# A two-layer encoder trunk: the scan's next operands are loaded after the head norm's store, and in the last head pair two kinds of load wait for steps of the chain

## The chip, the cores and the metric

The kernel runs on one core of a Trainium2 chip. A core has five engines, each with its own instruction queue that is worked through in order: TensorE (PE in the profile, with PEld for its weight loads), VectorE (DVE), ScalarE (ACT), GpSimd (POOL) and SyncE (SP). SyncE computes nothing here; it issues nearly all DMAs, so its queue is the order in which transfers begin. A DMA that waits for a semaphore holds up every DMA behind it in that queue. The metric is the device time of one execution in microseconds.

## The reference

The input x is 512 tokens by 1024 channels. Layer 0 is windowed attention with 16 heads, layer 1 is RWKV-7 time mixing with a forward and a backward scan; each is followed by a gated FFN with a convolution over three tokens. The change touches the time mixing alone, whose core is

```
step:  sa    = state @ a_t
       state = state * w_t + sa (x) b_t + v_t (x) k_t
       y_t   = state @ r_t
y   = scan(forward) + scan(backward)
out = (groupnorm(y) * lnx_w + lnx_b + bonus) * g
x   = x + out @ w_o
```

with 16 heads of 64 channels, all in float32.

## The kernel before, in words

The heads go two at a time, as a pair of 128 channels, so the scan has eight pairs (0 to 7). A pair's 512 tokens are cut into eight chunks of 64, and the chunked form needs, before the chain of steps can run: masked products of the operands (`low`, line 934, masked on VectorE at line 936 into tile `bw`), the inverse of 32 triangular blocks (`solve`, lines 998 and 1000, alternating between GpSimd and VectorE; its input `X` and its result go through DRAM as `ls` and `zs`, since they change partitions), two levels of matmuls with it (`inverses`, `level`), the sums over a pair's sides (`sides`, tile `xa`) and the batches of line 1069 and line 1078 (`batch`). Then eight steps (`step`) carry the state `st` from chunk to chunk: a matmul into a bank (line 1114), and a scaled copy on ScalarE (line 1117). Last is the head norm (`head_norm`, parts n0 to n4), whose result `t` part n4 stores to DRAM as `os` (line 1159).

These parts are laid out by hand. `run` goes over the pairs i, and for every step j it works through the words of `K.between[j]`: `c` is the step of pair i itself; `l0` to `l3` are `low` for pair i+2; `G`, `V` and `g` are rounds of `solve`; `n0` to `n4` are the norm of pair i-1; `p` (`prep`, lines 917 and 918) loads the operands `bk` and `ar` of pair i+3, 1 MB each, from DRAM. After `run`, all its instructions are tied together engine by engine, so that each engine, SyncE too, keeps the order in which they were written. Pair i+3, loaded in turn i, is first used by word `l0` in the first slot of turn i+1: the first of the matmuls at line 934 waits for both loads.

From turn 1 to turn 4 the turn has both a load (`p`) and a store (`n4`). Turns -1 and 0 load but have no norm, turn 5 and later have nothing left to load.

In the last turn (i = 7) `last` adds what the output projection needs: it loads x back from DRAM (`xs`, line 1414, 2 MB), and the generator `heads` loads the stored `os` of pair after pair (line 1424) and splits each into a high and a low part (`oh` on ScalarE, line 97, `ol` on VectorE), once per step from step 1 on. The projection's weights (`wo`, 448 KB each, loaded at line 55) are split likewise (`whi`, line 68; `wlo`, line 71). These weight blocks are written after `run` and are not tied to its order: the compiler's scheduler places their loads, casts and matmuls among the instructions of the last turn.

Of the kernel before, what the change touches and what calls it, by code (L numbers as in the profile page):

```python
# [11 lines left out]
AF = mybir.ActivationFunctionType  # L12
# [37 lines left out]
                        mybir.DependencyInfo(mybir.DependencyClass.NoSync, mybir.DependencyReason.DATA), reason="order")  # L50


def load(K, src, cols):
    raw = K.wraw.tile([P, 1024], F32, name="wraw")[:, :cols]
    K.nc.sync.dma_start(out=raw, in_=src)
    return raw


def weights(K, src, cols, lo_engine, raw=None):

    nc = K.nc
    if raw is None:
        raw = load(K, src, cols)
    hi = K.whi.tile([P, 1024], F32R, name="whi")[:, :cols]
    lo = K.wlo.tile([P, 1024], F32R, name="wlo")[:, :cols]
    K.nw += 1
    if K.wh[K.nw % len(K.wh)] == "C":
        nc.scalar.copy(out=hi, in_=raw)  # L68
    else:
        nc.vector.tensor_copy(out=hi, in_=raw)  # L70
    lo_engine.tensor_tensor(out=lo, in0=raw, in1=hi.bitcast(F32), op=ALU.subtract)  # L71
    return hi, lo


def ahead(K, blocks):

    raws = [load(K, *b[:2]) for b in blocks[:2]]
    nxt = weights(K, *blocks[0], raws[0])
    for i in range(len(blocks)):
        cur = nxt  # L80
        if i + 2 < len(blocks):
            raws.append(load(K, *blocks[i + 2][:2]))
        if i + 1 < len(blocks):
            nxt = weights(K, *blocks[i + 1], raws[i + 1])
        yield cur
# [10 lines left out]
def split(K, hi, lo, src, lo_engine):  # L96
    K.nc.scalar.copy(out=hi, in_=src)  # L97
    lo_engine.tensor_tensor(out=lo, in0=src, in1=hi.bitcast(F32), op=ALU.subtract)


def mm3(K, ps, lhs, rhs, first, last):

    nc = K.nc
    nc.tensor.matmul(ps, lhsT=lhs[0], rhs=rhs[0], start=first, stop=False)  # L104
    nc.tensor.matmul(ps, lhsT=lhs[0], rhs=rhs[1], start=False, stop=False)  # L105
    nc.tensor.matmul(ps, lhsT=lhs[1], rhs=rhs[0], start=False, stop=last)  # L106
# [709 lines left out]
def rwkv_scan(K, A, sc, mid):  # L816

    nc = K.nc
# [4 lines left out]
    C = nc.scalar  # L823
    R = Ctx()
# [6 lines left out]
    def er(e):  # L831
        return slice(HD * e, HD * e + HD)
# [14 lines left out]
    def mk(shape, name, bufs=1, dt=F32):  # L847
        pool = mid if name in MID else pools[next((k for k, v in PLACE.items() if name in v), "batch")]
        return pool.tile(shape, dt, name=name, tag=name, bufs=bufs)
# [234 lines left out]
    def places(j):  # L1084

        return (j, NC - 1 - j), (j, (NC - 1 - j) ^ 4)
# [11 lines left out]
    def added(ct, c, j):  # L1098

        cc, qq = places(j)  # L1100
        c.S = bank("ch", 2)[:, 0:P].rearrange("p (d s) -> p d s", d=2)
        for d, e in BOTH:
            T.matmul(c.S[er(e), d], lhsT=c.BW[:, qq[d], d, e, P:], rhs=c.VV[:, qq[d], d, e], start=d == 0, stop=j == 0 and d == 1)

    def step(ct, c, j):

        cc, qq = places(j)
        st = c.st if j else None
        last = j == NC - 1
        if j == 0:  # L1110
            added(ct, c, 0)
        if not last:
            for d, e in BOTH if j else ():
                T.matmul(c.S[er(e), d], lhsT=c.MT[qq[d] // 4][er(e), qq[d] % 4, d], rhs=st[er(e), d], start=False, stop=d == 1)
            c.st = mk([P, 2, HD], "st", K.nst)
            for d in range(2):
                C.activation(out=c.st[:, d], in_=c.S[:, d], func=AF.Copy, scale=R.gc[:, ct, j, d:d + 1])
        for d, e in BOTH if j else ():
            T.matmul(c.Y[er(1 - e), cc[d]], lhsT=c.QT[qq[d] // 4][er(e), qq[d] % 4, d], rhs=st[er(e), d],
                     start=False, stop=last and d == 1)  # L1120
        if j < NC - 2:
            added(ct, c, j + 1)
# [142 lines left out]
def body(ctx, tc, A, out, stage=9):  # L1265
    nc = tc.nc
    K = Ctx()
    K.nc = nc
    K.tc = tc
    K.nf, K.no, K.nx1s, K.nbon, K.nslot2, K.nwa, K.nrk, K.nar, K.nbk, K.nrt, K.nbr, K.nl, K.nxa, K.nvv = 3, 5, 32, 2, 6, 1, 1, 2, 2, 2, 4, 2, 2, 2  # L1270
    K.nx, K.ntt, K.ntp, K.nak, K.nx1, K.nmt, K.nst, K.depth = 1, 2, 2, 1, 1, 1, 3, 1
    K.e_r = K.e_k = nc.gpsimd
# [42 lines left out]
    K.begin, K.tail = (2,), ("pl", "", "", "")  # L1315
    K.ny = 2
    K.eng.update(z0="V", z1="V")
    K.between = ("w0 c l0 l1 b0 u g4", "c l2 l3 b1 g4 z X I", "c m1 w1 n0 e", "c n1 t0 t1 G3", "c a0 p n2 V6", "c L0 n3 V6", "c L1 a1 n4 V5", "c x0 x1 m0 G4")
    const = ctx.enter_context(tc.tile_pool(name="const", bufs=1, reuse_waits="tile"))

    @contextmanager
    def streams(n, work=True, side="left", psum=True):
        with ExitStack() as e:
            K.wraw = e.enter_context(tc.tile_pool(name=f"wraw{n}", bufs=3, side=side, reuse_waits="tile"))
            K.whi = e.enter_context(tc.tile_pool(name=f"whi{n}", bufs=2, side=side, reuse_waits="tile"))
            K.wlo = e.enter_context(tc.tile_pool(name=f"wlo{n}", bufs=2, side=side, reuse_waits="tile"))
            if work:
                K.work = e.enter_context(tc.tile_pool(name=f"work{n}", bufs=1, reuse_waits="tile"))
            if psum:
                K.pmm = e.enter_context(tc.tile_pool(name=f"pmm{n}", bufs=2, side=side, space=PSUM, reuse_waits="tile"))  # L1330
            yield
# [41 lines left out]
    def right(name):  # L1373
        return tc.tile_pool(name=name, bufs=1, side="right", reuse_waits="tile")

    def ffn(layer, xT, st, nxt, nst, store):
        conv_ffn(K, layer, st["h"], st["l"], st["acc"], A[f"w_up{layer}"], A[f"w_down{layer}"],
                 residual(xT, nxt, nst, store))

    xs = dram.tile([KT, P, S], F32, name="xs")  # L1380
# [26 lines left out]
    with ExitStack() as end:  # L1407
        ops = ExitStack()

        def last(R):  # L1410

            R.x = end.enter_context(right("x1")).tile([P, KT, S], F32, name="xT")
            for i in range(4):
                nc.sync.dma_start(out=R.x[:, 2 * i:2 * i + 2], in_=xs[2 * i:2 * i + 2].rearrange("k p s -> p k s"))
            end.enter_context(streams(2, False, "right", False))
            hl = ops.enter_context(right("ohl"))
            R.oh = [hl.tile([P, S], F32R, name=f"oh{i}") for i in range(KT)]
            R.ol = [hl.tile([P, S], F32R, name=f"ol{i}") for i in range(KT)]


            def heads():
                for i in range(KT - 1):
                    t = hl.tile([P, S], F32, name="o", tag="o", bufs=2)
                    nc.sync.dma_start(out=t, in_=sc["o"][i])
                    split(K, R.oh[i], R.ol[i], t, nc.vector)
                    yield

            return heads()

        scan.run(last)  # L1430
        xT = scan.x
        n = KT - 1
        for ot, (hi, lo) in enumerate(ahead(K, [(A["wo"][i], n * P, nc.vector) for i in range(KT)])):
            ps = scan.bank()
            for kt in range(n):
                c = slice(kt * P, (kt + 1) * P)
                mm3(K, ps, (hi[:, c], lo[:, c]), (scan.oh[kt], scan.ol[kt]), kt == 0, kt == n - 1)
            nc.vector.tensor_tensor(out=xT[:, ot], in0=xT[:, ot], in1=ps, op=ALU.add)
        hi, lo = weights(K, A["wo7"], KT * P, nc.vector)
        left.close()  # L1440
        with tc.tile_pool(name="act2", bufs=1, reuse_waits="tile") as K.act:
            K.accp = K.work = K.act
            on_tile = residual(xT, "nch1" if stage > 2 else None, st if stage > 2 else None, out if stage == 2 else None)
            for ot in range(KT):
                ps = scan.bank()
                c = slice(ot * P, (ot + 1) * P)
                mm3(K, ps, (hi[:, c], lo[:, c]), (scan.oh[n], scan.ol[n]), True, True)
                on_tile(ot, ps)
            ops.close()
            scan.pre.close()  # L1450
            if stage > 2:
                with tc.tile_pool(name="work2", bufs=1, reuse_waits="tile") as K.work:
                    ffn(1, xT, st, None, None, out)
# [75 lines left out]
```

## Time and profile before

| | |
|---|---|
| median of 3 runs | 1610.0 us (1609.33 to 1611.05) |
| the profiled execution's own time | 1609.2 us |
| its span, first to last instruction | 1607.0 us |
| mean granted TensorE clock | 0.942 of full speed |
| PE busy | 1482.1 us, 92% of the span |
| DVE, ACT, POOL busy | 1033.8, 688.2, 442.5 us |
| DMA | 179.09 MB, 111 GB/s on average |

The span has three parts. Up to about 720 us, and again from about 1226 us on, the big matmuls of attention, projections and FFN keep PE at 90% and more. In between lie the preparation of the scan and the eight turns. The first step of turns 0 to 7 begins at 928.6, 961.1, 994.1, 1026.4, 1062.1, 1096.7, 1130.6 and 1170.6 us. In the turns no engine is full: of the 33.0 us from 961.1 to 994.1 PE is busy for 26.95, DVE for 23.47, ACT for 13.97 and POOL for 11.30. A busy share tells little there; what tells is which wait ends last.

### The profile page before, as it was taken

Reading aid. Unit: us, or ns where it says so; the run is one execution under the profiler, and the core shown is the slowest. Engines: PE = TensorE matmul, PEld = TensorE weight load, DVE = VectorE, ACT = ScalarE, POOL = GpSimd, SP = SyncE. Lnnn points to the kernel's source line nnn. Section 1 sums busy time; section 2 is a strip of 40 time slices with the busy share of each in tenths; the row PEclk is TensorE's granted clock in tenths of the full one; section 3 lists DMA queues with packets and bytes.
Section 4 is the critical chain, followed back from the end, with each engine's and each line's share of the span. In section 5 each row is a group of like instructions: output and inputs, shape, how many; then the busy total and the mean of one; then the engine's idle time right before and its main releaser. Section 6 shows DMA issues by size and latency. Waiting matters only on the chain. (4 is left out here: it accounts for less than half of the span.)

```text
span 1607.0 us, 28495 instructions
## 1 busy us (share of the span) xinstructions
PE 1482.1 (92%) x11612; PEld 1197.7 (75%) x11612; DVE 1033.8 (64%) x1642; ACT 688.2 (43%) x1227; POOL 442.5 (28%) x533
## 2 busy tenths in 40 slices
PE   8999999999999998989986588888699999999999
PEld 7767688888888886767765477777577788888887
DVE  6876447777773348968987657667256677777222
ACT  5576534444432224556544243434344444444111
POOL 2630003222310015425498323322200333221000
PEclk9999999999999999999986589877889999999999
DMA  5200022333333322446536546764532222323331
GB/s 189 78 27 1 13 93 92 102 95 101 96 99 115 99 95 66 133 153 216 186 142 200 168 107 148 157 159 112 172 111 79 92 93 92 103 94 102 105 118 56
DMA packets 108978, 179.09 MB, mean 111 GB/s; under 512 B 49200, under 2 KB 62128, under 8 KB 108848
## 3 DMA queue, kind: packets, MB, share of 16 engines
q1 hardware_dynamic: 108704, 177.27, 36.5%
q8 instruction: 91, 1.49, 0.4%
q14 instruction: 39, 0.32, 0.1%
q10 hardware_dynamic: 144, 0.00, 0.0%
HBM read 142.91 MB, written 34.34 MB: 110 GB/s over the span
## 5 line engine op out<-in xcount | busy, mean ns | idle before, releaser
L68 ACT CAST whi<-wraw 128x1024 fp32r<-128x1024 f32 (+2 forms) x196 | 200.4, 1023 | 275.6 <-PE mm L105 179.7
L71 DVE TENSOR_TENSOR wlo<-wraw,whi 128x1024 fp32r<-128x1024 f32 (+2 forms) x139 | 166.9, 1201 | 183.1 <-ACT whi L68 182.3
L104 PE MATMUL mm<-hl,whi 128*128 128x512 f32 x720 | 281.2, 391 | 1.5 <-DVE xT L1359 0.9
L106 PE MATMUL mm<-hl,wlo 128*128 128x512 f32 x720 | 281.6, 391 | 0.5 <-POOL wlo L71 0.4
L105 PE MATMUL mm<-hl,whi 128*128 128x512 f32 x720 | 281.0, 391 | 0.4 <-DVE hl L92 0.4
L71 POOL TENSOR_TENSOR wlo<-wraw,whi 128x1024 fp32r<-128x1024 f32 x57 | 137.1, 2405 | 413.0 <-ACT whi L68 413.0
L185 DVE SCALAR_TENSOR_TENSOR conv<-upad,par,conv 128x512 f32<-128x512 f32 x88 | 125.6, 1430 | 64.0 <-ACT conv L182 64.0
L106 PEld LDWEIGHTS mm<-hl,wlo 128*128 128x128 f32 x720 | 135.5, 188 | 32.0 <-POOL wlo L71 2.7
L104 PEld LDWEIGHTS mm<-hl,whi 128*128 128x128 f32 x720 | 135.6, 188 | 29.7 <-ACT hl L91 1.3
L105 PEld LDWEIGHTS mm<-hl,whi 128*128 128x128 f32 x720 | 135.5, 188 | 29.3 <-DVE hl L92 1.1
L106 PE MATMUL mm<-gh,wlo 128*128 128x512 f32 x352 | 139.0, 395 | 0.0
L104 PE MATMUL mm<-gh,whi 128*128 128x512 f32 x352 | 139.0, 395 | 0.0
L105 PE MATMUL mm<-gl,whi 128*128 128x512 f32 x352 | 139.0, 395 | 0.0
L97 ACT CAST gh<-gact 128x512 fp32r<-128x512 f32 x44 | 27.3, 621 | 141.3 <-DVE gact L194 141.3
L182 ACT ACTIVATE conv<-upad,par 128x512 f32<-128x512 f32 x88 | 71.6, 815 | 21.5 <-DVE upad L180 21.3
L105 PEld LDWEIGHTS mm<-gl,whi 128*128 128x128 f32 x352 | 66.1, 188 | 16.1
L106 PEld LDWEIGHTS mm<-gh,wlo 128*128 128x128 f32 x352 | 66.1, 188 | 16.1
L998 POOL TENSOR_TENSOR tg<-X,Y 128x56 f32<-128x56 f32 (+16 forms) x129 | 47.2, 366 | 111.7 <-DVE Y L1000 81.2
L104 PEld LDWEIGHTS mm<-gh,whi 128*128 128x128 f32 x352 | 66.1, 188 | 15.9
L187 DVE SCALAR_TENSOR_TENSOR conv<-upad,par,conv 128x512 f32<-128x512 f32 x88 | 70.0, 798 | 3.0
L192 ACT ACTIVATE silu<-conv 128x512 f32<-128x512 f32 x44 | 27.8, 632 | 91.3 <-DVE conv L187 91.3
L106 PE MATMUL mm<-sx,wlo 128*128 128x512 f32 (+1 forms) x144 | 58.8, 409 | 2.9 <-DVE wlo L71 2.9
(334 smaller groups left out, 3110.2 us busy)
## 6 DMA issues: line engine op xcount, KB each, us to landing
wraw<-in_w_up_dram SPq DMA_DIRECT2D x88, 512.0 KB, 3.6
wraw<-in_w_down_dram SPq DMA_DIRECT2D x32, 512.0 KB, 3.5
ars<-tab SPq DMA_DIRECT2D x16, 512.0 KB, 3.0
bks<-tab SPq DMA_DIRECT2D x16, 512.0 KB, 3.2
ar<-ars SPq DMA_DIRECT2D x8, 1024.0 KB, 8.7
bk<-bks SPq DMA_DIRECT2D x8, 1024.0 KB, 6.7
wraw<-in_w_down_dram SPq DMA_DIRECT2D x16, 384.0 KB, 3.2
wraw<-in_w_qkv_dram SPq DMA_DIRECT2D x11, 512.0 KB, 4.3
```

What stands on the lines that cost most here:

```text
L68: nc.scalar.copy(out=hi, in_=raw)
L71: lo_engine.tensor_tensor(out=lo, in0=raw, in1=hi.bitcast(F32), op=ALU.subtract)
L97: K.nc.scalar.copy(out=hi, in_=src)
L104: nc.tensor.matmul(ps, lhsT=lhs[0], rhs=rhs[0], start=first, stop=False)
L105: nc.tensor.matmul(ps, lhsT=lhs[0], rhs=rhs[1], start=False, stop=False)
L106: nc.tensor.matmul(ps, lhsT=lhs[1], rhs=rhs[0], start=False, stop=last)
L182: nc.scalar.activation(out=c, in_=u[:, 1:S + 1], func=AF.Identity, scale=K.par[:, cw + 2 * FT + ch:cw + 2 * FT + ch + 1], bias=K.par[:, cb ...
L185: nc.vector.scalar_tensor_tensor(out=c, in0=u[:, 0:S], scalar=K.par[:, cw + ch:cw + ch + 1], in1=c, op0=ALU.mult, op1=ALU.add)
L187: nc.vector.scalar_tensor_tensor(out=c, in0=u[:, 2:S + 2], scalar=K.par[:, cw + 4 * FT + ch:cw + 4 * FT + ch + 1], in1=c, op0=ALU.mult, op ...
L192: nc.scalar.activation(out=sg, in_=acts[0], func=AF.Silu)
L998: en.tensor_tensor(out=tm, in0=X[:, 0:kx, kx:kx + 1].broadcast_to([P, kx, n]), in1=Y[:, kx:kx + 1, m:16].broadcast_to([P, kx, n]), op=ALU. ...
```

## The change

There are two parts.

First, the word `p` moves from slot 4 of `K.between` to slot 6, behind `n4`. It issues DMAs alone, so no other engine's order changes by it; in SyncE's queue the loads of `bk` and `ar` now stand behind the store `os` of the same turn.

Second, in the last turn. A helper `paced` makes a DMA wait for a given instruction. `step` notes its latest scaled copy of the state as `R.pace`. The load of x, formerly four DMAs ahead of everything, becomes four DMAs inside `heads`: two of the eight tiles of x behind step 1, two behind step 3, two behind step 5 and two behind step 6 (step 7 makes no state). The first three loads of output weights wait for steps 2, 4 and 6, through the list `K.paces`.

```
+def paced(K, later, earlier):
+
+    K.tc.add_manual_dep(later.ins, earlier.ins.name,
+                        mybir.DependencyInfo(mybir.DependencyClass.Sync, mybir.DependencyReason.DATA), reason="pace")
...
 def load(K, src, cols):
     raw = K.wraw.tile([P, 1024], F32, name="wraw")[:, :cols]
-    K.nc.sync.dma_start(out=raw, in_=src)
+    x = K.nc.sync.dma_start(out=raw, in_=src)
+    if K.paces:
+        paced(K, x, K.paces.pop(0))
     return raw
...
-                C.activation(out=c.st[:, d], in_=c.S[:, d], func=AF.Copy, scale=R.gc[:, ct, j, d:d + 1])
+                R.pace = C.activation(out=c.st[:, d], in_=c.S[:, d], func=AF.Copy, scale=R.gc[:, ct, j, d:d + 1])
...
-    K.between = (... "c a0 p n2 V6", "c L0 n3 V6", "c L1 a1 n4 V5", "c x0 x1 m0 G4")
+    K.between = (... "c a0 n2 V6", "c L0 n3 V6", "c L1 a1 n4 p V5", "c x0 x1 m0 G4")
...
             R.x = end.enter_context(right("x1")).tile([P, KT, S], F32, name="xT")
-            for i in range(4):
-                nc.sync.dma_start(out=R.x[:, 2 * i:2 * i + 2], in_=xs[2 * i:2 * i + 2].rearrange("k p s -> p k s"))
...
                     split(K, R.oh[i], R.ol[i], t, nc.vector)
+                    if i % 2 == 0:
+                        paced(K, nc.sync.dma_start(out=R.x[:, i:i + 2], in_=xs[i:i + 2].rearrange("k p s -> p k s")), R.pace)
+                    else:
+                        K.paces.append(R.pace)
                     yield
```

What the built programs' queues show. SyncE's queue in turn 1, before: the loads of a pair's `bk` and `ar` stand between the loads for the norm (`gt`, `bo`) and the norm's store `os`; `ls` is the first store of the next turn.

```order
L1055 DMA gt<-gs 128x512 [waits DMAHW0_49]
L1057 DMA bo<-bos 128x512 [waits DMAHW1_49]
L917 DMA bk_5951<-bks 128x2x1024 [waits DMAHW2_49,PE_49]
L918 DMA ar_7303<-ars 128x2x1024 [waits DMAHW3_49,DVE_49]
L1159 DMA os<-t 128x512 [waits DMAHW4_49,DVE_49]
L942 DMA ls<-bw_7305 32x16x32 [waits DMAHW5_49,DVE_49]
```

The same place now (lines above the change have moved on by 6 or 8):

```order
L1063 DMA gt<-gs 128x512 [waits DMAHW0_49]
L1065 DMA bo<-bos 128x512 [waits DMAHW1_49]
L1167 DMA os<-t 128x512 [waits DMAHW2_49,DVE_49]
L925 DMA bk_5951<-bks 128x2x1024 [waits DMAHW3_49,PE_49]
L926 DMA ar_7303<-ars 128x2x1024 [waits DMAHW4_49]
L950 DMA ls<-bw_7305 32x16x32 [waits DMAHW5_49,DVE_49]
```

The store, which waits for VectorE, now stands ahead of both loads. The same swap is in turns 2, 3 and 4 and nowhere else.

SyncE's queue at the start of the last turn, before (`xT<-xs` is x, `o<-os` a stored pair, `wraw<-in_wo_dram` a block of output weights):

```order
L1159 DMA os<-t 128x512 [waits DMAHW5_49,DVE_49]
L1414 DMA xT<-xs 128x2x512 [waits PE_49,DMAHW6_49,Activation_49,Pool_49]
L1414 DMA xT<-xs 128x2x512 [waits DMAHW7_49]
L1414 DMA xT<-xs 128x2x512 [waits DMAHW0_49]
L1414 DMA xT<-xs 128x2x512 [waits DMAHW1_49]
L1424 DMA o<-os 128x512 [waits DMAHW2_49]
L1055 DMA gt<-gs 128x512 [waits DMAHW3_49]
L1057 DMA bo<-bos 128x512 [waits DMAHW4_49]
L1424 DMA o<-os 128x512 [waits DMAHW5_49]
L55 DMA wraw<-in_wo_dram 128x896 [waits DMAHW6_49]
L55 DMA wraw<-in_wo_dram 128x896 [waits DMAHW7_49]
L55 DMA wraw<-in_wo_dram 128x896 [waits DMAHW0_49]
```

And now, from the DMA behind that `os` on:

```order
L1431 DMA o<-os 128x512 [waits DMAHW6_49,PE_49]
L1434 DMA xT<-xs 128x2x512 [waits PE_49,DMAHW7_49,Activation_49,Pool_49]
L1063 DMA gt<-gs 128x512 [waits DMAHW3_49,DMAHW0_49]
L1065 DMA bo<-bos 128x512 [waits DMAHW4_49,DMAHW1_49]
L1431 DMA o<-os 128x512 [waits DMAHW2_49]
L1431 DMA o<-os 128x512 [waits DMAHW6_49,DVE_49]
L61 DMA wraw<-in_wo_dram 128x896 [waits Activation_49]
L1434 DMA xT<-xs 128x2x512 [waits DMAHW5_49,Activation_49]
L1431 DMA o<-os 128x512 [waits DMAHW2_49,DVE_49]
L1431 DMA o<-os 128x512 [waits DMAHW7_49,DMAHW3_49,DVE_49]
L61 DMA wraw<-in_wo_dram 128x896 [waits DMAHW0_49,Activation_49]
L1434 DMA xT<-xs 128x2x512 [waits DMAHW1_49,Activation_49]
```

The four loads of x are spread out, each with its wait for a step on ScalarE (`Activation`), and the loads of `o` and of weights stand behind them.

ScalarE's queue at the same place, before (`x_...` and `vv` are the copies between the two batches, `st` the states of the steps, `t<-t` a square in the norm):

```order
L904 COPY x_11840<-mm 128x4x64
L68 CAST whi<-wraw 128x896
L904 COPY x_11840<-mm 128x4x64
L904 COPY vv<-mm 64x4x64 x4
L68 CAST whi<-wraw 128x896
L904 COPY x_11865<-pre_5948 128x4x64
L904 COPY x_11865<-pre_5949 128x4x64
L904 COPY vv<-pre_5948 64x4x64 x2
L904 COPY vv<-pre_5949 64x4x64 x2
L1117 ACTIVATE st<-bank,gc 128x64 x4
L97 CAST oh_11930<-o 128x512
L1117 ACTIVATE st<-bank,gc 128x64 x2
```

And now, up to step 4:

```order
L912 COPY x_11840<-mm 128x4x64 x2
L912 COPY vv<-mm 64x4x64 x4
L912 COPY x_11865<-pre_5948 128x4x64
L912 COPY x_11865<-pre_5949 128x4x64
L1125 ACTIVATE st<-bank,gc 128x64 x4
L105 CAST oh_11926<-o 128x512
L1125 ACTIVATE st<-bank,gc 128x64 x2
L105 CAST oh_11927<-o 128x512
L76 CAST whi<-wraw 128x896
L1125 ACTIVATE st<-bank,gc 128x64 x2
L1148 ACTIVATE t<-t 128x512
L105 CAST oh_11928<-o 128x512
```

The two weight casts have left the copies ahead of step 0; the first now stands between steps 2 and 3, the second (not shown) between steps 4 and 5.

## Rows read from the trace of the kernel before

**Rows 1.** Timeline of SyncE, turns 1 to 4: start us, issue us, line, DMA

```profile
978.86 0.38 SPq L917 DMA_DIRECT2D bk<-bks  x1
979.33 0.42 SPq L918 DMA_DIRECT2D ar<-ars  x1
988.81 0.33 SPq L1159 DMA_DIRECT2D os<-t  x1
...
1021.46 0.33 SPq L1159 DMA_DIRECT2D os<-t  x1
...
1054.13 0.33 SPq L1159 DMA_DIRECT2D os<-t  x1
...
1089.32 0.33 SPq L1159 DMA_DIRECT2D os<-t  x1
```

**Rows 2.** DMA view, load at 979.33 (KB, us to landing); then all of line 918

```profile
ar<-ars SPq DMA_DIRECT2D x1, 1024.0 KB, 8.7
...
DMA to landing us min/median/max: 5.2/8.7/10.5
```

**Rows 3.** Timeline of PE: the first masked product of turns 2 to 5

```profile
994.11 0.49 PE L934 MATMUL mm<-ar,bk 64*128 64x128 f32 x4
...
1026.49 0.38 PE L934 MATMUL pre<-ar,bk 64*128 64x128 f32 x2
...
1062.16 0.49 PE L934 MATMUL mm<-ar,bk 64*128 64x128 f32 x4
...
1096.74 0.49 PE L934 MATMUL pre<-ar,bk 64*128 64x128 f32 x4
```

**Rows 4.** Timeline of DVE, turns 2 to 4: copy behind the masks [idle before <-releaser]

```profile
1000.95 0.59 DVE L906 COPY X<-Y 64x512 f32<-64x512 f32 x1 [0.39 <-POOL Y L1000]
...
1033.59 0.59 DVE L906 COPY X<-Y 64x512 f32<-64x512 f32 x1 [0.66 <-POOL Y L1000]
...
1068.64 0.59 DVE L906 COPY X<-Y 64x512 f32<-64x512 f32 x1
```

**Rows 5.** Chain that ended last, turn 1: start us, us, what

```profile
968.05 0.59 DVE X L906
...
972.80 5.13 DMA X<-ls
...
988.09 0.69 DVE t L1155
```

**Rows 6.** Chain that ended last, start of the last turn

```profile
1154.96 8.69 DMA wraw<-in_wo_dram
```

**Rows 7.** Timeline of ACT, last pair

```profile
1153.78 0.37 ACT L904 COPY x<-mm 128x256 f32<-128x256 f32 x1 [1.17 <-PE mm L1069]
1163.73 0.94 ACT L68 CAST whi<-wraw 128x896 fp32r<-128x896 f32 x1 [9.58 <-DMA wraw<-in_wo_dram]
1164.57 0.36 ACT L904 COPY x<-mm 128x256 f32<-128x256 f32 x1
...
1170.61 0.52 ACT L1117 ACTIVATE st<-bank,gc 128x64 f32<-128x64 f32 x2 [1.24 <-PE bank L1103]
...
1175.64 0.52 ACT L1117 ACTIVATE st<-bank,gc 128x64 f32<-128x64 f32 x2 [1.98 <-PE bank L1114]
...
1179.38 0.52 ACT L1117 ACTIVATE st<-bank,gc 128x64 f32<-128x64 f32 x2 [1.16 <-PE bank L1114]
...
1181.99 0.52 ACT L1117 ACTIVATE st<-bank,gc 128x64 f32<-128x64 f32 x2 [1.09 <-PE bank L1114]
```

**Rows 8.** Timeline of PE, last pair: the two batches of line 1078

```profile
1165.63 2.74 PE L1078 MATMUL mm<-bw,x 64*64 64x128 f32 x32 [11.01 <-ACT vv L904]
...
1172.96 1.10 PE L1078 MATMUL pre<-bw,x 64*64 64x128 f32 x32
```

**Rows 9.** Busy us by stretch: PE, PEld, DVE, ACT, POOL, then granted clock, DMA share, GB/s

```profile
1159.90:1165.60 5.70, 0.00 (x0) 0.00 (x0) 0.90 (x1) 1.84 (x4) 0.00 (x0) 0.50 0.78 300
```

**Rows 10.** DMA view: a weight load issued at 1165.82 (KB, us to landing)

```profile
wraw<-in_wo_dram SPq DMA_DIRECT2D x1, 448.0 KB, 3.2
```

More of the change, by code (lines that the diff above doesn't have):

```diff
@@ L1269, in body @@
     K.tc = tc
+    K.paces = []
     K.nf, K.no, K.nx1s, K.nbon, K.nslot2, K.nwa, K.nrk, K.nar, K.nbk, K.nrt, K.nbr, K.nl, K.nxa, K.nvv = 3, 5, 32, 2, 6, 1, 1, 2, 2, 2, 4, 2, 2, 2
@@ L1317, in body @@
     K.eng.update(z0="V", z1="V")
-    K.between = ("w0 c l0 l1 b0 u g4", "c l2 l3 b1 g4 z X I", "c m1 w1 n0 e", "c n1 t0 t1 G3", "c a0 p n2 V6", "c L0 n3 V6", "c L1 a1 n4 V5", "c x0 x1 m0 G4")
+    K.between = ("w0 c l0 l1 b0 u g4", "c l2 l3 b1 g4 z X I", "c m1 w1 n0 e", "c n1 t0 t1 G3", "c a0 n2 V6", "c L0 n3 V6", "c L1 a1 n4 p V5", "c x0 x1 m0 G4")
     const = ctx.enter_context(tc.tile_pool(name="const", bufs=1, reuse_waits="tile"))
```

## The prediction

> **What bounds the kernel now.** I read the chain of waits first, then the timelines of the engines that it names. In the turns the chain runs through the inverse of the triangular blocks: masked products on PE, masks on DVE, the store `ls`, its way back as `X` (5.13 us), the rounds of `solve`, and behind them the norm's last product `t` at 1155, which `os` stores [rows 5]. SyncE's timeline shows the two loads going out about 10 us ahead of that store, 978.86 and 979.33 against 988.81 in turn 1 [rows 1]. PE's timeline shows where they are used: line 934 begins 5.30, 5.03, 8.03 and 7.42 us behind `os` in the four turns [rows 1, 3], and waits for no DMA, since `ar` had landed at 979.33 + 8.7 = 988.0 [rows 1, 2], six us before.
>
> In the last turn the chain rests on a weight load of 8.69 us [rows 6], because on ScalarE the cast of that weight block stands between two copies that step 0 needs: the first copy ends at 1154.15, the cast waits 9.58 us, the second copy comes at 1164.57 [rows 7]. PE does nothing for 11.01 us [rows 8], and in a part of that stretch the granted clock is 0.50, the 1.2 GHz level, with 300 GB/s of DMA and no matmul [rows 9]. The 32 matmuls that follow take 2.74 us; the same 32 later take 1.10 [rows 8].
>
> **The change, part by part. The loads of the next pair.** Nothing is added or removed, and both loads pass one DMA in one queue, which itself waits for VectorE. So they go out behind `os`: its start, 0.33 of issue and a gap make 0.4; then 0.47 from the one issue to the other and 8.7 to landing [rows 1, 2], 9.2 together. Line 934 then can't begin before `os` + 9.6. (Before, two loads of 256 KB were just ahead of the pair of loads, now a store of 256 KB is; I leave the 8.7.) Before it began 5.30, 5.03, 8.03 and 7.42 behind `os`, so in every turn the wait ends later than what now releases it. Nothing covers it: PE takes its queue in order, and behind that matmul stand the masks, `ls`, `X`, the solve, the norm and the next `os`.
>
> The delays accumulate turn by turn, because the next `os` hangs on the late matmul. From line 934 to the next `os` it took 27.35, 27.64 and 27.16 us [rows 1, 3]. One slack is in this: the copy behind the masks waited for POOL by 0.39 and 0.66 us in turns 2 and 3 and not at all in turn 4 [rows 4], so that a late PE first eats that.
> - Turn 2: 988.81 + 9.6 = 998.4, late by 4.3. Next `os` late by 4.3 - 0.4 = 3.9, at 1025.4.
> - Turn 3: 1025.4 + 9.6 = 1035.0, late by 8.5. Next `os` late by 7.85, at 1062.0.
> - Turn 4: 1062.0 + 9.6 = 1071.6, late by 9.4. Next `os` late by 9.4, at 1098.7.
> - Turn 5: 1098.7 + 9.6 = 1108.3, late by 11.6.
>
> Turn 5 loads nothing, so the 11.6 us stay until the end. Bounds: the quickest landing of line 918 was 5.2, the slowest 10.5 [rows 2]. With 5.2, line 934 can begin at `os` + 6.1: late by 0.8 and 1.5 in turns 2 and 3 and never in the others beyond what is carried, in all +0.9. With 10.5 it is 1.8 more in each of four turns, +19 with the slack gone. I take 8.7, since the 10 us that the loads of turn 1 had were measured at this very place.
>
> On the size of a transfer a rule speaks lower. The trace has two loads of 1 MB landed 9.2 us after the first was issued [rows 1, 2]. The Trainium skill ("DMA: Bandwidth & Descriptors", section "Anatomy of one DMA — SWDGE (gpsimd) path") gives a fit for another path of issue than SyncE's: about 2.0 us and the bytes at 436 GB/s. By it, as an estimate, 2 MB land in 6.8 us, `os` + 7.2, and the whole would be +3.0 instead of +11.6. The trace doesn't agree, and its 9.2 decides; the lower figure is a rival below.
>
> **The last pair.** The weight cast leaves ScalarE's copies, so the second copy follows the first: 1164.57 - 1154.15 = 10.4 us earlier. From it to step 0 (1170.61) took 6.0 us [rows 7], with one more cast (0.94) and a batch at the lower clock (2.74 for 1.10) in it; without these I take 4.5, so step 0 is at 1158.7 and step 1 about 1.0 later (all on the old clock, without the first part's delay). How much of this lead stays is set by the waits that the change adds. ScalarE now has the first weight cast between steps 2 and 3. Its load waits for step 2, and ahead of it in SyncE's queue stand x (from step 1 on), `gt`, `bo` and two loads of `o`, at 0.33 to 0.42 us of issue each, some 0.5 with the gap [rows 1]: step 1 at 1159.7, x out at 1160.2, the weights out at 1162.8. A weight load by itself lands in 3.2 us [rows 10], one behind 3 MB of others in 8.7 [rows 6]; here about half of that is in front, and I take 5.0. So it lands at 1167.8, is cast in 0.94, and step 3 comes at 1168.8 instead of 1175.64: 6.8 of the 10.4 us are left. The second cast stands between steps 4 and 5, and its load waits for step 4, behind the issue of an `o`: step 4 is 3.74 us behind step 3 [rows 7], 1172.5, then 0.5 + 0.5 + 3.2 + 0.94 and the start of step 5, 0.5: 1178.1 instead of 1181.99. That leaves 3.9 us. Behind step 6 stand more projection matmuls than before (27 instead of 12), but PE was to have done these in the waits between steps and they still depend on the same casts; I keep 4.0 us as the gain of this part.
>
> Bounds: if the loads land so that no cast waits, the whole 10.4 stays, and with the batch at the higher clock (2.74 - 1.10) and a cast gone it is -12.9. If each of the casts costs what the longest load does (8.7 for 5.0 and for 3.2), 3.7 and 5.5 more, 9.2 in all, a gain of 4.0 turns into a loss of 5.2; with half of the 9.2 it is a loss of 0.6, and that is my end, since the x loads no longer stand in front in one block. x itself is read only at the projection's end, behind step 6; its last part is issued with step 6 and lands in a few us beside the 27 matmuls, so I cost it at nothing, and at 3 us if they are quicker than I think.
>
> The first matmuls of the FFN behind it stand in a slightly different order, the same in number: 0, within 1 us.
>
> **Sum.** 1609.2 (the profiled execution) + 11.6 - 4.0 = 1616.8. It was 0.8 us under the median of 1610.0, so 1617.5 us.
>
> **The rivals.**
>
> *The loads land sooner than I take it (faster).* Behind `os` the queues are empty, and the loads share them with nothing. For it: `ar` landed in 5.2 us once [rows 2]. With 0.9 for the first part and -4.0 for the second the kernel runs in 1606.9; the sum falls below before as soon as both loads have landed some 7 us after the first issue. By the estimate from the Trainium skill above it would be +3.0 - 4.0, 1609.0. Against it: 2 MB stand there, not one, and the median is 8.7. 13%.
>
> *The last pair gives back its whole wait.* The casts then find their weights landed, and 11.6 - 12.9 makes 1608.7, no change. For it: a weight load takes only 3.2 us alone. Against it: each of them waits for a step and the cast stands before the next. 10%.
>
> *The clock falls too.* PE now has nothing to do for some 4 us more in front of line 934, in four turns. What the trace shows of this is the stretch without PE work at a granted clock of 0.50, and a batch of 2.74 us where 1.10 was due [rows 8, 9]. That batch lost 1.64 us by it. If in each of the four turns as much as one or two such batches of the first products run at the lower level, 1.6 to 3.3 us are lost a turn; with 2.3, 4 x 2.3 = 9 more, 1626. The Trainium skill ("TensorE: Matmul & The Clock Gate", section "Part 1: The HAM clock gate (the "warmup" mystery)") says that a TensorE left idle goes back to half its rate; the trace agrees, with 0.50 in that stretch [rows 9]. Against it: 4 us is under half of the 11 us gap of the last pair. 15%.
>
> *The scan doesn't feel the wait.* If another engine were what the next `os` waits for, PE's delay would vanish, and only the second part would act: 1609.2 - 4.0 + 0.8 = 1606.0. What speaks for it would be slack on POOL; there is 0.39, 0.66 and 0 [rows 4], too little for 4 us. 5%.
>
> **How the numbers follow.** Forecast 57% (its own range, with half a microsecond a landing in four turns and the second part between 0 and -8, is 1612 to 1623), sooner landing 13%, last pair's whole wait 10%, clock 15%, wait not felt 5%. A difference under 0.2%, 3.2 us, can't be told from none. Faster takes half of the sooner landing, the wait not felt and some of the last pair's case: 0.14. Same is the rest of these two: 0.14. Slower is the forecast and the clock: 0.72. The range runs from the sooner landing (1606) to the clock's case with a little more (1628).
>
> **What the profile after will show.** If the first part is right, line 934 waits for a DMA (`ar` or `bk`) in turns 2 to 5 and in no other, by about 4.3, 4.6, 1.6 and 2.2 us; it starts 9.6 behind each `os`; and the loads' landing is still 8 to 9 us. The waits of the copy for POOL are gone. If the clock's case is right, line 934's matmuls behind that wait take twice their time. If the second part is right, the cast's wait of 9.58 and PE's of 11.01 are gone, the batch takes about 1.1, the first cast has a wait of some us between steps 2 and 3, the second a shorter one between 4 and 5, and from the first copy of x to step 6 it is about 4 us less than before. The forecast is wrong if line 934 doesn't wait, if the loads land in 6 us or less, or if the time from the first x copy to the end of the projection has shrunk by more than 8 us or hasn't at all.

## The result, and the profile after

The changed kernel takes 1627.28 us (median of 5 runs, 1626.16 to 1628.34), the kernel before on the same chip 1611.05. The ratio is 1.0096, 95% interval 1.0079 to 1.0114: 0.96% slower, 13 to 18 us. Forecast were 1617.5 us and a range of 1606 to 1628. The sign was right and the time lies just inside the range, but the loss is 16.2 us between the medians where 7.5 were forecast, over twice as much. The profiled execution has a span of 1625.0 us, 18.0 more than before.

Where the 18.0 us arise is seen by setting the same instructions of the two traces beside each other:

| point | before, us | after, us | later by |
|---|---|---|---|
| step 0 of turn 1 | 961.1 | 960.6 | -0.5 |
| first product of `low` in turn 2 | 994.11 | 997.69 | 3.6 |
| in turn 5 | 1096.74 | 1110.62 | 13.9 |
| first copy of `x` in the last turn | 1153.78 | 1169.82 | 16.0 |
| step 0 of the last turn | 1170.61 | 1174.45 | 3.8 |
| step 6 | 1183.57 | 1195.86 | 12.3 |
| cast of pair 5's `o` | 1188.32 | 1204.77 | 16.5 |
| cast of the last pair (`oh<-t`) | 1207.70 | 1224.86 | 17.2 |
| end of the span | 1607.0 | 1625.0 | 18.0 |

So the turns lose 16 us, the last pair wins 12 of them at step 0, and everything is given back by the time that the last pair is cast.

*The loads behind the store.* SyncE's timeline, answering to [rows 1]; start, issue time, line, DMA:

```profile
988.62 0.32 SPq L1167 DMA_DIRECT2D os<-t  x1
989.03 0.38 SPq L925 DMA_DIRECT2D bk<-bks  x1
989.46 0.50 SPq L926 DMA_DIRECT2D ar<-ars  x1
...
1025.71 0.32 SPq L1167 DMA_DIRECT2D os<-t  x1
...
1062.95 0.32 SPq L1167 DMA_DIRECT2D os<-t  x1
...
1101.18 0.32 SPq L1167 DMA_DIRECT2D os<-t  x1
```

The loads of turn 1 go out 10 us later than before, 0.4 behind `os`. Their landing has hardly changed; the DMA view of all of line 926, answering to [rows 2]:

```profile
DMA to landing us min/median/max: 5.3/8.4/10.0
```

PE's timeline, the first products of turns 2 to 5, answering to [rows 3]; in brackets how long PE was idle ahead of them and for what:

```profile
997.69 1.22 PE L942 MATMUL mm<-ar,bk 64*128 64x128 f32 x13 [2.89 <-DMA ar<-ars]
...
1034.96 1.25 PE L942 MATMUL pre<-ar,bk 64*128 64x128 f32 x16 [4.24 <-DMA ar<-ars]
...
1072.55 0.71 PE L942 MATMUL mm<-ar,bk 64*128 64x128 f32 x8 [4.45 <-DMA ar<-ars]
...
1110.62 1.77 PE L942 MATMUL pre<-ar,bk 64*128 64x128 f32 x16 [4.96 <-DMA ar<-ars]
```

They begin 9.07, 9.25, 9.60 and 9.44 us behind `os`; before, they had waited for no DMA at all. In the chain that ended last the loads of `ar` now stand four times, where none stood before:

```profile
989.46 8.09 DMA ar<-ars
...
1026.56 8.27 DMA ar<-ars
...
1063.80 8.61 DMA ar<-ars
...
1102.03 8.46 DMA ar<-ars
```

What the waits do to PE's clock is seen in busy time by stretch (PE, PEld, DVE, ACT, POOL, granted clock, DMA share, GB/s), from the first product on. First before, in turns 2 and 5:

```profile
994.10:998.10 4.00, 4.00 (x79) 3.73 (x77) 2.52 (x6) 1.00 (x4) 3.29 (x10) 1.00 0.02 4
1096.70:1100.70 4.00, 4.00 (x79) 3.71 (x77) 2.48 (x4) 1.03 (x4) 3.14 (x12) 1.00 0.00 0
```

And after:

```profile
997.70:1003.20 5.50, 5.50 (x77) 5.09 (x79) 2.61 (x5) 0.52 (x2) 2.37 (x9) 0.69 0.03 6
1110.60:1116.10 5.50, 5.48 (x76) 5.14 (x78) 2.58 (x4) 0.52 (x2) 2.09 (x9) 0.69 0.00 0
```

For about as many matmuls (77 for 79) PE is busy 5.5 us instead of 4.0, at 0.69 of full speed on average, that is, partly at the 1.2 GHz level. The second pair of masked products shows it on VectorE, in turn 2 at 1003.17:

```profile
1003.17 1.29 DVE L944 TENSOR_TENSOR bw<-mm,mask 128x512 f32<-128x512 f32 x2 [1.01 <-PE mm L942]
```

That is 5.48 us behind the first product; in the other turns it is 5.44, 5.43 and 5.53, and before it was 3.96 or 3.97 in all four. The waits of VectorE for GpSimd behind the masks [rows 4] are gone, as foretold; turn 2's copy:

```profile
1005.68 0.59 DVE L914 COPY X<-Y 64x512 f32<-64x512 f32 x1
```

*The last pair.* ScalarE's timeline, answering to [rows 7]:

```profile
1169.82 0.65 ACT L912 COPY x<-mm 128x256 f32<-128x256 f32 x2 [1.36 <-PE mm L1077]
1174.45 0.52 ACT L1125 ACTIVATE st<-bank,gc 128x64 f32<-128x64 f32 x2 [0.50 <-PE bank L1111]
...
1183.07 0.62 ACT L105 CAST oh<-o 128x512 fp32r<-128x512 f32 x1 [6.08 <-DMA o<-os]
1184.92 0.94 ACT L76 CAST whi<-wraw 128x896 fp32r<-128x896 f32 x1 [1.23 <-DMA wraw<-in_wo_dram]
1185.76 0.51 ACT L1125 ACTIVATE st<-bank,gc 128x64 f32<-128x64 f32 x2
...
1194.01 0.94 ACT L76 CAST whi<-wraw 128x896 fp32r<-128x896 f32 x1 [2.29 <-DMA wraw<-in_wo_dram]
1194.86 0.51 ACT L1125 ACTIVATE st<-bank,gc 128x64 f32<-128x64 f32 x2
...
1195.86 0.52 ACT L1125 ACTIVATE st<-bank,gc 128x64 f32<-128x64 f32 x2
...
1204.77 0.62 ACT L105 CAST oh<-o 128x512 fp32r<-128x512 f32 x1 [8.38 <-DMA o<-os]
```

The two copies now come together (x2), step 0 follows in 4.6 us, and the cast's wait of 9.58 is gone. In its place stand waits between the steps, 6.08 for an `o` and 1.23 for the weights ahead of step 3, 2.29 ahead of step 5. Behind step 6 stands one of 8.38 for the `o` of pair 5. On PE there is a gap of 6.13 behind step 3, ahead of the first projection products (line 112), and one of 2.36 behind step 6:

```profile
1185.91 0.79 PE L112 MATMUL mm<-oh,whi 128*128 128x512 f32 x1 [6.13 <-ACT whi L76]
...
1205.44 0.73 PE L112 MATMUL mm<-oh,whi 128*128 128x512 f32 x2 [2.36 <-ACT oh L105]
```

Before, ScalarE's wait for that `o` was 4.23 and PE's gap behind step 6 was 2.07:

```profile
1188.32 0.62 ACT L97 CAST oh<-o 128x512 fp32r<-128x512 f32 x1 [4.23 <-DMA o<-os]
...
1188.99 0.73 PE L104 MATMUL mm<-oh,whi 128*128 128x512 f32 x2 [2.07 <-ACT oh L97]
```

The cast came 4.75 us behind step 6 before, and comes 8.91 behind it now. PE's gap has grown by only 0.3 because PE now has more projection matmuls to do there, and nine of them, from 1196.4 to 1199.4, run at a granted clock of 0.50; they end at 1203.1. The end of the last pair in the chain, before and then after:

```profile
1185.57 2.67 DMA o<-os
```

```profile
1178.40 6.44 DMA wraw<-in_wo_dram
...
1190.42 3.57 DMA wraw<-in_wo_dram
1198.52 6.17 DMA o<-os
```

The same load of pair 5's `o` takes 6.17 us instead of 2.67: ahead of it in the queues now stand the third part of x, sent behind step 5 at 1195.40, and two weight loads from 1196.41 on, put off to there by the paces.

### The profile page after: what moved, and what is told of

It is laid out like the page before. It is cut to its first block, busy times and chain, and to the rows that moved or that the text cites. A ratio compares the mean times of both kernels' runs of the same rounds, so it can differ in the third digit from the quotient of the medians.

```text
span 1625.0 us, 28503 instructions
## 1 busy us (share of the span) xinstructions
PE 1493.8 (92%) x11612; PEld 1205.3 (74%) x11612; DVE 1033.3 (64%) x1642; ACT 689.3 (42%) x1227; POOL 441.1 (27%) x533
## 4 chain that ended last, share of the span: by engine, by line
PE 68%; DVE 13%; DMA 6%; POOL 5%; issue 4%; ACT 3%; SPq 1%; DVEq 0%; POOLq 0%; ACTq 0%
PE mm L114 16%; PE mm L113 16%; PE mm L112 16%; DMA ar<-ars 2%; PE mm L395 2%; DVE wlo L79 2%; PE sc L113 2%; PE tp L390 2%; PE sc L112 2%; PE sc L114 1%; POOL Y L1008 1%; DMA X<-ls 1%; PE sc L375 1%; POOL tg L1006 1%; DVE bw L944 1%
## 5 line engine op out<-in xcount | busy, mean ns | idle before, releaser
L1125 ACT ACTIVATE st<-bank,gc 128x64 f32<-128x64 f32 x112 | 29.4, 317 | 80.7 <-PE bank L1122 76.8
```

What stands on the lines that cost most here:

```text
L1125: R.pace = C.activation(out=c.st[:, d], in_=c.S[:, d], func=AF.Copy, scale=R.gc[:, ct, j, d:d + 1])
```

## The experiments

Each ran beside the kernel before on its chip; two chips' medians are compared by their ratios alone.

**Only the loads.** The kernel before with the new `K.between`, nothing else.

```
+    K.between = (... "c a0 n2 V6", "c L0 n3 V6", "c L1 a1 n4 p V5", "c x0 x1 m0 G4")
```

> Only the word p moves; the last pair is as before. Theory: the loads behind the store are worth +16 us by the time the last pair begins (11.6 of waiting for the loads, the rest a lower clock behind each wait), so 16 over before, about 1627, the same as the whole change; first masked product 9.0 to 9.5 us behind os in turns 2 to 5. Rival, the prediction's own sizes: the loads cost 11.6 and the pacing adds 5, so 1622 to 1623 here.

Measured: 1627.46 us against 1610.1, ratio 1.0120 (1.0101 to 1.0139), 16 to 22 us slower. The first products come 8.74, 9.24, 9.39 and 9.42 us behind `os`. PE's timeline in turn 3, where the wait is the shortest of the four:

```profile
1032.27 1.16 PE L934 MATMUL pre<-ar,bk 64*128 64x128 f32 x16 [2.67 <-DMA ar<-ars]
```

The theory holds: this part alone makes the whole loss, and the prediction's own sizes (12) lie outside the interval. The excess over 16 is partly in this kernel's last turn, which has the old order and whose weight cast waited 10.74 us here instead of 9.58.

**Only the pacing.** The changed kernel with the old `K.between`.

> Only the last turn changes; p stays in slot 4. Theory: step 0 comes 12 us sooner behind the first copy of x, step 6 only 4 us sooner, and behind step 6 all of it is lost to projection matmuls that had filled the steps before and to the loads of o: +0 to +2 us over before. Rival, the prediction: a gain of 4.0 us.

Measured: 1611.12 against 1610.1, ratio 1.0008 (0.9996 to 1.0020). The gain of 4.0 us is ruled out; it is no change, or a loss of up to 3 us. In its trace, from the first copy of `x` to `oh<-t` it takes 55.45 us, against 53.92 before and 55.04 in the changed kernel.

**PE kept busy in the wait.** In the changed kernel, products of the identity into the banks that the first masked products overwrite.

```
         pvs = [bank().rearrange("p (c s) -> p c s", c=4) for _ in range(2)]
+        if g == 0:
+            for n in range(K.warm.get(ct, 0)):
+                T.matmul(pvs[n % 2][:, n // 2 % 4], lhsT=K.ident[er(n % 2), :], rhs=K.ident[er(n % 2), :], start=True, stop=True)
...
+    K.warm = {4: 36, 5: 50, 6: 56, 7: 60}
```

> The whole change, with 36, 50, 56 and 60 products of the identity on PE ahead of the first masked product in turns 2 to 5; their results are overwritten. Theory: PE stays at its higher clock through the wait, the second pair of masked products comes about 4.0 us behind the first instead of 5.5, and 3 to 6 us of the loss come back (1621 to 1624). Rival: the clock costs nothing here, what is beyond 11.6 comes from other queues: no change from the changed kernel (1627), or more by what the added products delay.

Measured: 1628.17 us, ratio 1.0126 (1.0105 to 1.0147): no gain. The size was wrong: the added products took 4.29 to 6.97 us, and three of the four times line 945, the first masked products, came with no wait for a DMA, 10.6 to 11.1 us behind `os`, one to two later than the loads would have let them. So the time of this run says nothing on the clock. With fewer:

> As the run with added products, but 22, 32, 33 and 37 of them, so that they end ahead of the landing (before, they ended up to 2 us behind it and gave back what they saved). Theory: the clock behind each wait stays up, the second pair of masked products follows the first by 4.0 instead of 5.5 us, four times 1 to 1.5 us come back: 1622 to 1624. Rival: the solve on VectorE and GpSimd sets the turn and the quicker products only wait: 1627 to 1628, as the changed kernel.

Measured: 1624.7 us, ratio 1.0077 (1.0059 to 1.0094). It points to the clock, but the interval overlaps with that of the changed kernel (1.0079 to 1.0114), on another chip. So both once more, on one chip:

> The changed kernel once more, on the chip of the next run, as its base: 15 to 18 us over before.

> The changed kernel with 22, 32, 33 and 37 products of the identity ahead of the first masked product of turns 2 to 5, on the same chip as the changed kernel. If the lower clock behind each wait is a part of the loss, 3 to 6 us under the changed kernel; if the turn is set elsewhere, within 1 us of it.

Measured: the changed kernel 1627.74 (1625.1 to 1630.86), ratio 1.0095 (1.0079 to 1.0111); with the added products 1623.65 (1623.0 to 1624.61), ratio 1.0073 (1.0061 to 1.0086). No run of the one reaches the other's. The medians are 4.1 us apart; by the spread of the five runs each, this is known to about 3 us, and by the two ratios it is 3.5. So some 4 us of the loss are the clock. The first product and the second pair of masks of turn 2, in this second trace of the changed kernel:

```profile
998.49 2.08 PE L942 MATMUL mm<-ar,bk 64*128 64x128 f32 x16 [4.79 <-DMA ar<-ars]
```

```profile
1004.92 1.29 DVE L944 TENSOR_TENSOR bw<-mm,mask 128x512 f32<-128x512 f32 x2 [1.36 <-PE mm L942]
```

That is 6.43 us, and 5.43, 6.08 and 6.47 in the other turns, at a granted clock of 0.57 to 0.69. PE and VectorE of the run with the added products, turn 3:

```profile
1031.23 3.84 PE L941 MATMUL pre<-ident 64*128 64x128 f32 x64
1036.17 1.16 PE L945 MATMUL pre<-ar,bk 64*128 64x128 f32 x16 [1.10 <-DMA ar<-ars]
1037.14 1.09 PE L945 MATMUL mm<-ar,bk 64*128 64x128 f32 x16
```

```profile
1040.13 1.29 DVE L947 TENSOR_TENSOR bw<-pre,mask 128x512 f32<-128x512 f32 x2 [0.26 <-PE pre L945]
```

The load still lands 9.1 us behind `os` (1027.05), so the wait itself is untouched, but the second pair of masks follows the first product by 3.96 us, as before the change, and in all four turns the granted clock is 1.00 for the 4 us from the first product on. PE does more work, and the kernel is quicker.

**Half the bytes behind the store.** The changed kernel, but `bk` is loaded in slot 4 as before (word `p`) and `ar` alone behind `n4` (a new word `r`), in turns 1 to 4. The lines that define `r` are left out here.

```
+    K.between = (... "c a0 p n2 V6", "c L0 n3 V6", "c L1 a1 n4 r V5", "c x0 x1 m0 G4")
```

> The whole change, but only the load of ar goes behind os; that of bk stays in slot 4 (turns 1 to 4). Theory: 1 MB instead of 2 lands 5 to 5.5 us behind its issue, os + 5.5 to 6, which is later than before by under 1 us in turns 2 and 3 and not at all in the others: +1 to +2 from this part, and up to 2 from the last turn, 1612 to 1615. Rival: what costs is standing behind os at all, not the bytes: half of the loss or more stays, 1619 or over.

Measured: 1611.15 us, ratio 1.0005 (0.9989 to 1.0022), a little under what was expected. Its first products, turns 2 and 3:

```profile
996.27 0.94 PE L947 MATMUL mm<-ar,bk 64*128 64x128 f32 x12 [1.94 <-DMA ar<-ars]
...
1029.58 0.68 PE L947 MATMUL pre<-ar,bk 64*128 64x128 f32 x7 [1.25 <-DMA ar<-ars]
```

They come 6.26 and 6.45 us behind `os` (990.01 and 1023.13), 5.73 and 5.87 in turns 4 and 5. PE still waits for a load in turns 2 to 4, but shortly, and the second pair of masks follows by 3.96 or 3.97 us in all four: no clock is lost. Standing behind the store is not dear as such; 2 MB behind it are.

**The store in another queue.** The changed kernel with `os` issued from ScalarE.

```
-                nc.sync.dma_start(out=sc["o"][ct], in_=z)
+                nc.scalar.dma_start(out=sc["o"][ct], in_=z)
```

> The whole change, but os is issued from ScalarE's queue instead of SyncE's, so that bk and ar don't stand behind it although p is written behind n4. Theory: the whole loss of the first part comes from standing behind a store that waits for VectorE; without it line 934's wait is gone and the time is that of the pacing alone, 1610 to 1613. Rival: the loads are late because of where p is written, or ScalarE loses as much by waiting for os: 1618 or over.

Measured: 1614.93 us against 1611.57, ratio 1.0020 (1.0008 to 1.0033). SyncE's queue and PE in turn 2 and at the start of turn 3:

```profile
1014.60 0.39 SPq L925 DMA_DIRECT2D bk<-bks  x1
```

```profile
1030.04 1.16 PE L942 MATMUL pre<-ar,bk 64*128 64x128 f32 x16
```

The loads go out 8 to 11 us ahead of `os` again (1023.39 in that turn). Line 942 waits for no DMA in any turn, and most of the loss is gone, though `p` is still written behind `n4`: it was the queue. Some 2 us more than with the pacing alone (1.0008) are left. The two intervals overlap, so this is not clear of the noise, and whether it is ScalarE's issues was not tried.

**The end of the last pair.** The run with the pacing alone, but x's third part goes behind the last `o`, and the third weight load waits for no step.

```
-                    if i % 2 == 0:
+                    if i in (0, 2, 6):
                         paced(K, nc.sync.dma_start(out=R.x[:, i:i + 2], ...), R.pace)
-                    else:
+                    if i == 6:
+                        paced(K, nc.sync.dma_start(out=R.x[:, 4:6], ...), R.pace)
+                    if i in (1, 3):
                         K.paces.append(R.pace)
```

> p in slot 4; the last turn as changed, but the third quarter of x is loaded behind the last o, and only the first two weight loads wait for steps, so that 1.4 MB less stand ahead of the load of pair 5's o. Theory: that o lands 2 to 3 us sooner behind os, but at most the 2.4 us for which PE waits for it come back: 1 to 2.4 under the run with the pacing alone, 1608.5 to 1610. Rival: the 15 more projection matmuls behind step 6 alone set the end: no change from it, 1611.

Measured: 1607.19 us against 1611.57, ratio 0.9972 (0.9959 to 0.9985), more than expected. ScalarE's cast of that `o` and PE's next products, first of the pacing alone, then of this run:

```profile
1189.80 0.62 ACT L105 CAST oh<-o 128x512 fp32r<-128x512 f32 x1 [8.07 <-DMA o<-os]
...
1190.47 0.79 PE L112 MATMUL mm<-oh,whi 128*128 128x512 f32 x1 [3.66 <-ACT oh L105]
```

```profile
1190.60 0.62 ACT L105 CAST oh<-o 128x512 fp32r<-128x512 f32 x1 [4.94 <-DMA o<-os]
...
1191.27 0.73 PE L112 MATMUL mm<-oh,whi 128*128 128x512 f32 x2 [0.50 <-ACT oh L105]
```

The `os` went out at 1183.44 and 1187.37, so the cast follows it by 6.4 us with the pacing alone and by 3.2 here; PE's gap of 3.66 becomes 0.50. The clock comes back with it: the 12 products from 1191.0 on take 4.70 us at a granted clock of 0.50 with the pacing alone, and here the 12 from 1191.3 on take 3.20 at 1.00. From the first copy of `x` to `oh<-t` it is 50.7 us instead of 55.45. Both kernels have the same 21 projection matmuls between step 6 and the gap, so these are not what ends last; the late `o` was.

**A version without paces.** `p` in slot 4; x in four parts behind the loads of `o` of pairs 1 to 4, no DMA waiting for a step, and the first two weight casts ordered behind steps 1 and 2.

```
+        x = nc.scalar.copy(out=hi, in_=raw)
+        if K.casts:
+            behind(K, x, K.casts.pop(0))
...
+                    if 1 <= i <= 4:
+                        k = 2 * i - 2
+                        nc.sync.dma_start(out=R.x[:, k:k + 2], in_=xs[k:k + 2].rearrange("k p s -> p k s"))
+                    if i < 2:
+                        K.casts.append(R.pace)
```

> p in slot 4; x in four parts behind the loads of o for pairs 1 to 4 and waiting for no step, the weight loads waiting for no step either, but the first two weight casts ordered on ScalarE behind steps 1 and 2. Theory: step 0 is 12 us sooner behind the first copy of x as in the change, the weights have landed when their casts come, the projection matmuls fill the steps as before, and 8 to 12 us are gained: 1599 to 1602. Rival: the bytes set the end (x, o and weights are the same 5 MB), the casts or the o's wait in their stead: 1607 or over.

Measured: 1604.76 us (1599.6 to 1610.21) against 1611.57, ratio 0.9955 (0.9937 to 0.9973), 4 to 10 us under before: faster than both kernels, between the two expectations. ScalarE:

```profile
1158.17 0.65 ACT L914 COPY x<-mm 128x256 f32<-128x256 f32 x2 [1.17 <-PE mm L1079]
1162.80 0.52 ACT L1127 ACTIVATE st<-bank,gc 128x64 f32<-128x64 f32 x2 [0.51 <-PE bank L1113]
...
1164.72 0.95 ACT L76 CAST whi<-wraw 128x896 fp32r<-128x896 f32 x1
...
1166.47 0.96 ACT L76 CAST whi<-wraw 128x896 fp32r<-128x896 f32 x1
...
1177.93 0.52 ACT L1127 ACTIVATE st<-bank,gc 128x64 f32<-128x64 f32 x2
```

Neither cast waits, and step 6 is 19.8 us behind the first copy, against 29.8 before and 26.0 in the changed kernel. From that copy to `oh<-t` it is 44.6 us instead of 53.9, so the last pair wins 9.3. This version does two things at once, it spreads x and it keeps back the casts instead of the loads; which of them brings how much was not taken apart.

## Why the prediction was right and wrong

Two terms of the sum failed. The lower clock behind the waits stood in it at nothing and is worth some 4 us, and the last pair stood in it at -4.0 and measured +1.3. Together these are 9.4 us, and 8.7 are missing between 7.5 and 16.2.

**The wait for the loads: right in its place, and in its size partly by luck.** Forecast were `os` + 9.6 and 11.6 us, that is, 12.6 of waits less 1.05 of slack on GpSimd. Measured are 9.07 to 9.60, and over what they were before these sum up to 3.77 + 4.22 + 1.57 + 2.02 = 11.6. So the waits were a little shorter than forecast, and the slack gave nothing back; the two errors cancel. The rival of quicker landing fell: in the changed kernel `ar` took 8.1 to 8.6 us, and with half the bytes the loss is gone, so the size of the transfer decides, as the sum had it. The lower figure by the Trainium skill ("DMA: Bandwidth & Descriptors", section "Anatomy of one DMA — SWDGE (gpsimd) path"), as an estimate 6.8 us for 2 MB, is not borne out: both loads had landed 8.5 to 9.0 us after the first was issued.

**The clock: it was named as a rival, at 15%, and it belonged in the sum.** The argument against it, that 4 us is under half of the gap of 11 us of the last pair, failed: gaps of 2.9 to 5.0 us were enough to have the products behind them at 0.69. The rival's price, 2.3 us a turn, was of the right order: the second pair of masks comes 1.5 us later than before in each turn of the changed kernel's first trace, and 1.5 to 2.5 later in its second, 6.0 and 8.6 us in four turns. Not all of this reached the next `os`: the way from line 942 to it is 28.02, 27.99 and 28.63 us, 0.67, 0.35 and 1.47 longer than before, and in the first two of these turns the waits for GpSimd, 0.39 and 0.66, are gone. The forecast had taken that slack off its 12.6 of waits and had the way shorter by it. By the runs on one chip the clock is worth 4.1 us, known to about 3. That idle time lowers TensorE's rate is also in the Trainium skill ("TensorE: Matmul & The Clock Gate", section "Part 1: The HAM clock gate (the "warmup" mystery)"); the trace agrees, with 1.00 before and 0.69 after in about the same work.

**The last pair: right up to step 6, wrong in the step "I keep 4.0 us as the gain of this part".** Behind the first copy of `x`, step 0 came 12.2 us sooner (forecast 10.4 and about 1.5), step 3 5.9 (6.8), step 5 3.2 (3.9) and step 6 3.75 (4.0). But the gain ended there. The working looked only at who reads x, and priced its last part at nothing, at 3 us at most. It did not ask what stands behind x and the weights in the queue once they are put off: the load of pair 5's `o`, which ends last there in both kernels. With x's third part and two weight loads ahead of it, it took 6.17 us instead of 2.67. The cast of that `o` lost 4.16 us against step 6, more than the lead of 3.75 that was left. In the changed kernel the wait is not all of this: PE's own matmuls behind step 6, 21 by the trace where 12 stood before (27 in the working, which priced them at nothing), ended only 2.36 us ahead of the products that need that `o`. The sign that the forecast gave for being wrong, that the time from the first copy of `x` to the end hasn't shrunk at all, came true: 55.04 us to `oh<-t`, before 53.92. The pacing is worth +1.3 us (-0.6 to +3.2) instead of -4.0. The tail run shows the cause: with x and one weight load out of that `o`'s way, the part turns into a gain of 4.5 us (2.4 to 6.6).

**The sum again.** 11.6 for the waits, 4.1 for the clock and 1.3 for the last pair make 17.0, against 16.2 measured. The rivals of a scan that does not feel the wait and of the whole 12.9 us kept are out; the version without paces comes to 9.3 of these 12.9. The FFN's start, priced at 0 within 1 us, has 0.8 in the table above, from `oh<-t` to the end; no run took it apart.

What stays open is the length of single turns: the kernel before itself ran from 1604.3 to 1616.9 us on one of the chips, and a turn of the changed kernel, from `os` to `os`, differs by up to 1.7 us between its two traces (38.01 and 39.68 in the longest). For this the sizes here hold to some 2 or 3 us and no better.

## What to carry to other kernels

When a load is moved behind a store that waits for an engine, the price is the load's whole landing less the slack that the first reader had, once per turn if the next store hangs on that reader; then add the lower clock of what PE does behind the new gap. When transfers are put off to make room for one, list what is issued in the place they are put off to: the gain lasts until the first of these is what ends last. And try to order the instruction that was in the way (here the cast) rather than delay the load that it reads; here the version that did so, with x spread as well, was the fastest.

## What the runs showed of the hardware

A gap of 2.89 us on PE, and one of 2.67 in the run with only the loads moved, was already followed by 5.5 us at 0.69 of the full clock, while gaps of 1.25 to 1.94 us, in the run with half the bytes, cost nothing to be seen. No limit follows from this: in the last pair of the kernel before, the products behind a gap of 2.07 us ran at 0.93 for 1.9 us and then at 0.50 for 2.6. Filling the gap with useless products, 44 to 74 of them as the trace counts, made the kernel some 4 us faster. And 2 MB in two loads took 8.5 to 9.0 us from the first issue, while one of 1 MB behind the same store landed in 5.2 to 5.9 us.
